# Where two stages of a decoder layer keep their kept weights and sums of x: new offsets mod 512 bytes

## The chip, the cores and the metric

The kernel runs on one core of one Trainium2 chip. The metric is the time of one execution on the device, in microseconds, as the median of several runs. The profile is that of one further execution of the same program.

## What is computed

A decoder layer on 512 tokens of width 1024 in float32: a half-step SwiGLU block, a token mixer (two kinds of recurrent heads), and a second half-step SwiGLU block, each between two RMS norms. The change touches the first matrix product of the two SwiGLU blocks only:

```python
def swiglu_ffn(x, w_in, w_out):
    gate, up = jnp.split(x @ w_in, 2, axis=-1)
    return (jax.nn.silu(gate) * up) @ w_out

x = x + 0.5 * rms_norm(swiglu_ffn(rms_norm(x, norm_pre[l, 0]), ffn1_w_in[l], ffn1_w_out[l]), norm_post[l, 0])
...
x = x + 0.5 * rms_norm(swiglu_ffn(rms_norm(x, norm_pre[l, 2]), ffn2_w_in[l], ffn2_w_out[l]), norm_post[l, 2])
```

`w_in` is 1024 x 5632 (gate and up, 2816 columns each), `w_out` is 2816 x 1024.

## The kernel before, in words

**High and low parts.** Every float32 operand of a matrix product is split into a high part, rounded to the matmul's float32r, and a low part, the rest. A product is then three passes: high x high, high x low, low x high. In `split` (L188) and `cast` (L227) ScalarE writes the high part of a weight (L232) and VectorE the low part (L233); for x, `part` and `sums` do the same (L308, L310, L321, L322).

**The first product by halves.** `x @ w_in` is cut 2 x 2: tokens in halves of 256, the 1024 rows of `w_in` in halves of 512, and for a step t of 256 columns the gate's and the up's columns. From t = 1 on, seven products p1 to p7 with sums and differences of the four quarters stand for eight plain ones. The sums of the weights are made by GpSimd in place (L220), those of x once per block by `sums` (L315). For t = 0 the eight plain products are done: c1 to c4 on the first half of the tokens, e1 to e4 on the second half with the same four weights.

**One product** is `prod` (L496): 24 matmuls at L509, three passes of eight, and each matmul has 128 x 128 weights (the stationary operand, loaded by a LDWEIGHTS) and 256 columns of x (the moving operand). The passes are (weight high, x high), (weight high, x low), (weight low, x high); only c1 has the last two in the other order. Within a pass, the four k of one half of the columns run first and then the four k of the other. `after` (L524) combines what is in PSUM.

**The order** is written out by hand in `ORDER` (L41 to L49). The head (`HEADS`) is c1, c3, c2, c4, p1 of t = 1, e1, e3, e2, p1 of t = 2, p2 of t = 1, e4, p2 of t = 2. Then come p7, p5, p3, p6 of t = 1, the products of t = 2, and from t = 3 to t = 10 a fixed round of seven (p1, p4 of the step before, p3, p5, p7, p6, p2). p4 of t = 10 is done among the second product's matmuls. Transposes of x on TensorE (L288, plain float32) stand inside the head: in the first block between c2 and c4 and between c4 and p1, in the second between c1 and c3 and between c2 and c4. In the first block a transpose of 36 rows of small parameters (L966) stands between the last product of the head and p7 of t = 1.

**Where the operands lie.** Weights go to a ring of four slots in the tile `w`, except those of c1, c3 and c4, which are kept for e1, e3 and e4 in the three tiles `sq` (`self.stay`, chosen by `stay = {"c1": 1, "c3": 2, "c4": 0}` in `ffn_items`). Later the sums of x overwrite these tiles (`self.sq`): tile 0 for p3, tile 1 for p7, tile 2 for p6. The moving operands of all other products lie in the four tiles `xq`. Offsets below are word numbers (4 bytes) mod 128, so mod 512 bytes, in the program's memory: `w` slots begin at 120, all `xq` parts at 40, and the `sq` tiles begin at 56. `LATE` = 112 and `NEAR` = 48 are added to that. So before the change:

| operand | high part at | low part at |
|---|---|---|
| weights in the ring `w` (c2/e2 and p1 to p7) | 120 | 120 |
| kept weight of c1/e1 (`stay[1]`) | 56 | 104 |
| kept weights of c3/e3, c4/e4 (`stay[2]`, `stay[0]`) | 56 | 56 |
| x in `xq` (c1 to c4, e1 to e4, p1, p2, p4, p5) | 40 | 40 |
| sums of x for p3 and p6 (`sq[0]`, `sq[2]`) | 40 | 40 |
| sum of x for p7 (`sq[1]`) | 40 | 56 |

The kept weights are made in `split` with `dst` set; other weights take the next free slot there. `open_ffn` runs once for each block and places all this anew.

Of the kernel before, what the change touches and what calls it, by code (L numbers as in the profile page):

```python
# [16 lines left out]
D = 1024  # L17
# [2 lines left out]
ND = D // P  # L20
NF = FF // P
EPS = 1e-6
RAW, WBUF, PAD, LATE, NEAR = 3, 4, 128, 112, 48
PAIRS = NF // 2
HALF = T // 2
KH = ND // 2
# [18 lines left out]
for _t in range(HEAD, PAIRS):  # L45
    if _t == HEAD:
        ORDER += [("p1", _t), ("p3", _t), ("p5", _t), ("p4", _t - 1)] + [(p, _t) for p in ("p7", "p6", "p2")]
    else:
        ORDER += [("p1", _t), ("p4", _t - 1)] + [(p, _t) for p in ("p3", "p5", "p7", "p6", "p2")]  # L49


class Load:


    def __init__(self, key, src, a, b, ring="raw", depth=3, ahead=3, group=None):
        self.key, self.src, self.a, self.b, self.ring, self.depth, self.ahead = key, src, a, b, ring, depth, ahead
        self.group = group


class Item:  # L60

    def __init__(self, key, loads, rows=None, adds=(), dst=None, then=None, late=None, defer=False):
        self.key, self.loads, self.rows, self.adds, self.dst, self.then, self.late = key, loads, rows, adds, dst, then, late
        self.defer = defer
        self.reads = {key, *(k for pair in adds for k in pair)}


class Layer:  # L70
# [117 lines left out]
    def split(self):  # L188

        nc = self.nc  # L190
        it = self.items.popleft()
        raw = self.raw[it.key]
        _, a, b = raw.shape
        if it.dst:
            w = it.dst()
        else:
            if self.wt is None:
                self.wt = self.wp.tile([P, (2 * D + 128) * WBUF], F32R, name="w")

            n = self.free.popleft()  # L200
            o = PAD + (2 * D + 128) * n - 16 * (it.late if it.late is not None else b == 512)
            w = self.wt[:, o : o + 2 * D].rearrange("p (b k t) -> p b k t", b=2, k=a)
            self.slot[id(w)] = n, w
        hi, lo = self.both(w)
        self.ready.append((w, it.dst is not None))
        rows = it.rows
        if rows is None:
            yield from self.cast(hi, lo, raw, it.defer)
        else:
            for j in range(a):  # L210
                nc.scalar.activation(hi[:, j], raw[:, j], AF.Copy, scale=rows[:, j : j + 1])
            yield
            for j in range(a):
                nc.vector.scalar_tensor_tensor(
                    lo[:, j], raw[:, j], rows[:, j : j + 1], hi[:, j].bitcast(F32), op0=ALU.mult, op1=ALU.subtract
                )
        with self.behind(*self.hold):
            for out, other in it.adds:
                o, c = self.raw[out], self.raw[other]
                nc.gpsimd.tensor_tensor(o, o, c, op=ALU.add)  # L220
        if it.then:
            it.then(raw)
        self.load_due(self.done)
        self.done += 1
        yield
# [76 lines left out]
    def part(self, i, h, src):  # L302

        pv = self.turn(src, h)
        v = slice(i * P, (i + 1) * P)
        dst = self.xq[h][:, :, :, v]
        yield
        self.nc.scalar.copy(dst[:, 0], pv)  # L308
        yield
        self.nc.vector.tensor_tensor(dst[:, 1], pv, dst[:, 0].bitcast(F32), op=ALU.subtract)  # L310
        yield
        self.nc.scalar.copy(self.xf[h][:, :, v], pv)
        yield
# [163 lines left out]
    def open_ffn(self, ctx):  # L477

        hp = self.hpool = ctx.enter_context(self.tc.tile_pool(name=self.name("hp"), bufs=1))
        self.hf = hp.tile([P, NF, T], F32, name=self.name("hf"))  # L480
        self.xf = [self.hf[:, j : j + 2, :].rearrange("p a (b t) -> p (a b) t", t=HALF) for j in (NF - 4, NF - 2)]
        sq = [hp.tile([P, 2 * D + PAD], F32R, tag="s", bufs=3, name=self.name("sq")) for _ in range(3)]
        self.sq = [self.place(t, KH, True) for t in sq]

        part = lambda o: sq[1][:, o : o + D].rearrange("p (k t) -> p k t", k=KH)
        self.sq = [self.both(self.sq[0]), (part(D + LATE), part(0)), self.both(self.sq[2])]
        xq = [self.both(x) for x in self.xq]
        self.stay = [self.place(t, KH) for t in sq]
        self.stay[1] = (self.stay[1][:, 0], sq[1][:, D + NEAR : 2 * D + NEAR].rearrange("p (k t) -> p k t", k=KH))
        self.left = {"p1": xq[0], "p2": xq[1], "p4": xq[3], "p5": xq[2], "p6": self.sq[2], "p7": self.sq[1], "p3": self.sq[0]}  # L490
        self.left.update({"c1": xq[0], "c2": xq[1], "c3": xq[0], "c4": xq[1]})
        self.left.update({"e1": xq[2], "e2": xq[3], "e3": xq[2], "e4": xq[3]})
        self.gs, self.held, self.copies = [], {}, []
        self.hs, self.bank, self.later, self.u, self.q, self.had = deque(), {}, deque(), {}, {}, set()
# [106 lines left out]
    def start(self, norm, xn):  # L601
# [8 lines left out]
        split = self.split()  # L610
        step(q[1][0], q[1][1])
        next(split)
        step(q[1][0])
        next(split)
        step(q[0][0], q[1][0])
        head = deque(HEADS)
# [273 lines left out]
    def ffn_items(self, name, w_in, w_out):  # L890

        made = []
        place = {"p1": "a", "p2": "c", "p3": "d", "p4": "a", "p5": "a", "p6": "a", "p7": "b"}
        place.update({"c1": "a", "c2": "c", "c3": "b", "c4": "d"})
        adds = {}
        for t in range(1, PAIRS):
            if t >= HEAD:
                v1, v3 = ("p1", t), ("p4", t - 1)
            elif t > 1:
                v1, v3 = ("p3", t - 1), ("p6", t - 1)  # L900
            else:
                v1, v3 = ("p1", 1), ("p1", 2)
            for at, o, i in ((("p5", t), "a", "d"), (("p6", t), "a", "c"), (v1, "a", "b"), (v3, "b", "d")):
                adds.setdefault(at, []).append(((name, t, o), (name, t, i)))

        def load(t, r, group=None):
            ring = ("raw", 3) if t % 2 == 0 and r != "c" else ("raw2", 5)
            k, c = int(r in "cd"), int(r in "bd")
            c0 = c * FF + t * 2 * P
            src = w_in[k * 4 * P : (k + 1) * 4 * P, c0 : c0 + 2 * P].rearrange("(k p) f -> p k f", p=P)  # L910
            return Load((name, t, r), src, KH, 2 * P, *ring, 8, group)

        own = {("p1", t): [load(t, r) for r in "abdc"] for t in range(2, PAIRS)}
        own["c1", 0] = [load(t, r, None if (t, r) == (0, "d") else name) for t in range(2) for r in "acbd"]

        stay = {"c1": 1, "c3": 2, "c4": 0}
        for p, t in ORDER:
            if p[0] == "e":
                continue
            dst = (lambda n=stay[p]: self.stay[n]) if p in stay else None  # L920
            made.append(Item((name, t, place[p]), own.get((p, t), ()), None, adds.get((p, t), ()), dst))
        for h in range(2):
            for n, k2, kind in self.outs(h):
                src = w_out[k2 * 2 * P : (k2 + 1) * 2 * P, h * 512 : (h + 1) * 512].rearrange("(k p) d -> p k d", p=P)
                key = (name, "out", h, k2)
                made.append(Item(key, [Load(key, src, 2, 512, "raw2", 5, 8)], then=self.w_sums if kind in "kbs" else None, late=1 + (kind in "kbs")))
                if kind in "kbs":
                    made.append(Item(key, (), late=2, defer=True))
                if h == n == 0:
                    made.append(Item((name, PAIRS - 1, "a"), ()))  # L930
        return made
# [736 lines left out]
```

## Time and profile before

| | us |
|---|---|
| median of 3 runs | 935.06 (934.9 to 936.83) |
| the profiled execution | 934.93 |
| its span | 932.9 |
| TensorE busy | 921.9 (99%) |
| LDWEIGHTS busy | 856.8 (92%) |
| VectorE busy | 759.9 (81%) |
| ScalarE busy | 480.8 (52%) |
| GpSimd busy | 289.4 (31%) |

The profile names engines PE (matmuls), PEld (the loads of their weights, which overlap PE), DVE (VectorE), ACT (ScalarE), POOL (GpSimd), and a line by L and its number. A group of instructions is shown as output<-inputs by tile names, partitions x elements, and a count. Matmuls are pipelined: one that lasts 276 ns in the profile may start 113 ns after the one before it. So the time of a stretch is read from the starts of its first matmul and of the first one behind it, not from the sum of the durations. A row of the timeline ends some 0.16 us behind the start of the next row for the same reason.

### The profile page before, as it was taken

How to read it: one execution, taken by the hardware profiler on the slowest of the kernel's cores; microseconds unless marked ns; L12 is line 12 of the kernel's file. 1: busy time of each engine (PE TensorE's matmuls, PEld its weight loads, DVE VectorE, ACT ScalarE, POOL GpSimd, SP SyncE). 2: the span in 40 equal slices, each digit the busy share in tenths (PEclk: the TensorE clock that was granted, in tenths of full speed). 3: DMA queues.
4: the chain of work that ended last, by engine and by line, in shares of the span. 5: the costliest groups of instructions: out<-in, count | busy, mean ns of one | idle time of the engine just before them, and what ended most of it. 6: DMA issues, size and time to landing. Idle time of an engine off the chain costs nothing.

```text
span 932.9 us, 17378 instructions
## 1 busy us (share of the span) xinstructions
PE 921.9 (99%) x7239; PEld 856.8 (92%) x7239; DVE 759.9 (81%) x899; ACT 480.8 (52%) x653; POOL 289.4 (31%) x225
## 2 busy tenths in 40 slices
PE   9999999999999999999999999999999999999997
PEld 7999999999888879998888888999999999988885
DVE  6798999999768766788766665887999999976874
ACT  7644445444544544987753254853545445544441
POOL 3535555662000028000021301354555565100001
PEclk9999999999999999999999999999999999999999
DMA  9243334332323304432423126214324332233302
GB/s 315 92 136 114 113 92 136 118 110 68 109 95 98 106 1 116 113 91 70 137 69 114 46 90 204 90 27 133 114 91 136 114 113 92 68 115 99 104 23 91
DMA packets 81994, 97.14 MB, mean 104 GB/s; under 512 B 4178, under 2 KB 61558, under 8 KB 81915
## 3 DMA queue, kind: packets, MB, share of 16 engines
q1 hardware_dynamic: 81306, 94.44, 33.3%
q8 instruction: 57, 0.93, 0.4%
q0 software_dynamic: 320, 1.06, 0.3%
q10 hardware_dynamic: 288, 0.52, 0.2%
q14 instruction: 23, 0.18, 0.1%
HBM read 93.90 MB, written 2.11 MB: 103 GB/s over the span
## 4 chain that ended last, share of the span: by engine, by line
PE 61%; DVE 1%; POOL 0%; ACT 0%; issue 0%; DVEq 0%; POOLq 0%; ACTq 0%
PE ps L509 23%; PE ps L129 8%; PE ps L131 8%; PE ps L130 8%; PE ps L454 6%; PE ps L738 3%; PE ps L1167 1%; PE ps L464 1%; PE ps L288 1%; PE ps L1437 0%; PE ps L1405 0%; PE ps L1240 0%; PE ps L1206 0%; PE ps L1407 0%; PE ps L1361 0%; PE ps L1430 0%
## 5 line engine op out<-in xcount | busy, mean ns | idle before, releaser
L233 DVE TENSOR_TENSOR w<-raw,w 128x1024 fp32r<-128x1024 f32 x226 | 374.2, 1666 | 60.8 <-ACT w L232 60.4
L232 ACT CAST w<-raw 128x1024 fp32r<-128x1024 f32 x226 | 235.6, 1051 | 269.8 <-POOL raw L220 92.7
L220 POOL TENSOR_TENSOR raw<-raw,raw 128x1024 f32<-128x1024 f32 x80 | 221.1, 2764 | 175.0 <-DVE w L233 164.5
L509 PE MATMUL ps<-xq,w 128*128 128x256 f32 x2016 | 238.0, 277 | 0.0
L509 PEld LDWEIGHTS ps<-xq,w 128*128 128x128 f32 x2016 | 233.6, 188 | 0.2
L509 PE MATMUL ps<-sq,w 128*128 128x256 f32 x1440 | 171.0, 277 | 0.0
L509 PEld LDWEIGHTS ps<-sq,w 128*128 128x128 f32 x1440 | 167.4, 188 | 0.0
L129 PE MATMUL ps<-w,hs 128*128 128x512 f32 x240 | 93.5, 390 | 0.0
L130 PE MATMUL ps<-w,hs 128*128 128x512 f32 x240 | 93.5, 390 | 0.0
L131 PE MATMUL ps<-w,hs 128*128 128x512 f32 x240 | 93.5, 389 | 0.0
L129 PE MATMUL ps<-w,xq 128*128 128x512 f32 x208 | 83.1, 400 | 0.1
L130 PE MATMUL ps<-w,xq 128*128 128x512 f32 x208 | 81.0, 390 | 0.0
L131 PE MATMUL ps<-w,xq 128*128 128x512 f32 x208 | 81.0, 391 | 0.0
L375 POOL TENSOR_SCALAR col<-col 128x1 f32<-128x1 f32 x24 | 9.7, 403 | 204.3 <-ACT junk L374 204.3
L454 PE MATMUL ps<-xq,w 128*128 128x256 f32 x480 | 55.8, 278 | 0.0
L454 PEld LDWEIGHTS ps<-xq,w 128*128 128x128 f32 x480 | 55.4, 188 | 0.2 <-issue 0.2
L131 PEld LDWEIGHTS ps<-w,hs 128*128 128x128 f32 x240 | 45.1, 188 | 9.4
L129 PEld LDWEIGHTS ps<-w,hs 128*128 128x128 f32 x240 | 45.1, 188 | 8.7
L130 PEld LDWEIGHTS ps<-w,hs 128*128 128x128 f32 x240 | 45.1, 188 | 8.7
L131 PEld LDWEIGHTS ps<-w,xq 128*128 128x128 f32 x208 | 39.0, 188 | 8.7 <-DVE xq L295 0.3
L129 PEld LDWEIGHTS ps<-w,xq 128*128 128x128 f32 x208 | 39.1, 188 | 8.6 <-ACT xq L294 0.7
L130 PEld LDWEIGHTS ps<-w,xq 128*128 128x128 f32 x208 | 39.1, 188 | 7.5
(246 smaller groups left out, 1100.8 us busy)
## 6 DMA issues: line engine op xcount, KB each, us to landing
raw<-in_ffn_w_in_dram SPq DMA_DIRECT2D x88, 512.0 KB, 4.5
raw<-in_ffn_w_out_dram SPq DMA_DIRECT2D x44, 512.0 KB, 3.9
raw<-in_w_mix_in_dram SPq DMA_DIRECT2D x28, 512.0 KB, 4.0
raw<-in_w_mix_out_dram SPq DMA_DIRECT2D x8, 512.0 KB, 3.9
out_dram<-xs SPq DMA_DIRECT2D x8, 256.0 KB, 2.1
xs<-in_x_dram SPq DMA_DIRECT2D x6, 256.0 KB, 6.7
gpost<-in_norm_post_dram SPq DMA_DIRECT2D x3, 512.0 KB
gpre<-in_norm_pre_dram SPq DMA_DIRECT2D x2, 512.0 KB, 4.1
```

What stands on the lines that cost most here:

```text
L129: mm(ps, sh, mh, start=start, stop=False, **kw)
L130: mm(ps, sh, ml, start=False, stop=False, **kw)
L131: mm(ps, sl, mh, start=False, stop=stop, **kw)
L220: nc.gpsimd.tensor_tensor(o, o, c, op=ALU.add)
L232: lambda: nc.scalar.copy(hi, src),
L233: lambda: nc.vector.tensor_tensor(lo, src, hi.bitcast(F32), op=ALU.subtract),
L288: self.nc.tensor.transpose(pt[:, c * P : (c + 1) * P], src[:, k * P : (k + 1) * P], self.ident)
L375: nc.gpsimd.tensor_scalar(m, ss, s2 / D, b, op0=ALU.mult, op1=ALU.add)
L454: mm(ps[:, u0:u1], w[:, a, k, :], self.xop(k, b, u0, u1), start=k + n + m == 0, stop=k == ND - 1 and n == 2, skip_group_check=True,)
L464: self.nc.tensor.matmul(ps[:, :HALF], w[:, a, k, :], self.xop(k, b, 0, HALF), start=m + k == 0, stop=m == 2 and k == ND - 1)
L509: self.nc.tensor.matmul(ps[:, c], wb[b][:, k, v], left[d][:, k, :], start=first and a + n + k == 0, stop=n == 2 and k == KH - 1, skip_grou ...
L738: self.nc.tensor.matmul(out, a[:, x, ka, tok(qa, t)], b[:, y, kb, col(qb)], start=fresh and t + m == 0, stop=stop and m == 2, skip_group_c ...
```

## The change

It moves operands, and nothing else: which instructions run, in which order and on which data stays as it was.

- The kept weights go from the beginning of the `sq` tiles to `FAR` = 64 words behind it, so from 56 to 120, where the ring's weights lie. That of c1/e1 has its high part at 120 and its low part at 104 as before (it changes places with the high part inside the tile).
- All sums of x lie at 40: p7's low part goes from 56 to 40.
- `APART` names p1 of t = 4 and p1 of t = 7. Their weights have the high part in the second half of their slot, at 120, and the low part 16 words ahead of the slot's begin, at 104.

After it, every weight part lies at 120 and every x part at 40, but for four low parts of weights at 104: c1/e1's and those of the two p1.

```diff
-RAW, WBUF, PAD, LATE, NEAR = 3, 4, 128, 112, 48
+RAW, WBUF, PAD, LATE, NEAR, FAR = 3, 4, 128, 112, 48, 64
...
+APART = (("p1", 4), ("p1", 7))
...
-    def __init__(self, key, loads, rows=None, adds=(), dst=None, then=None, late=None, defer=False):
+    def __init__(self, key, loads, rows=None, adds=(), dst=None, then=None, late=None, defer=False, apart=False):
+        self.apart = apart
...
             w = self.wt[:, o : o + 2 * D].rearrange("p (b k t) -> p b k t", b=2, k=a)
+            if it.apart:
+                w = tuple(self.wt[:, v : v + D].rearrange("p (k t) -> p k t", k=a) for v in (o + D, o - 16))
...
-        part = lambda o: sq[1][:, o : o + D].rearrange("p (k t) -> p k t", k=KH)
-        self.sq = [self.both(self.sq[0]), (part(D + LATE), part(0)), self.both(self.sq[2])]
+        part = lambda t, o: t[:, o : o + D].rearrange("p (k t) -> p k t", k=KH)
+        self.sq = [self.both(x) for x in self.sq]
+        self.stay = [(part(t, FAR), part(t, D + FAR)) for t in sq]
+        self.stay[1] = part(sq[1], D + FAR), part(sq[1], NEAR)
         xq = [self.both(x) for x in self.xq]
-        self.stay = [self.place(t, KH) for t in sq]
-        self.stay[1] = (self.stay[1][:, 0], sq[1][:, D + NEAR : 2 * D + NEAR].rearrange("p (k t) -> p k t", k=KH))
...
-            made.append(Item((name, t, place[p]), own.get((p, t), ()), None, adds.get((p, t), ()), dst))
+            made.append(Item((name, t, place[p]), own.get((p, t), ()), None, adds.get((p, t), ()), dst, apart=(p, t) in APART))
```

## The prediction

> **What bounds the kernel now.** I read the page first, for who is busy and what ends the waits of the matmuls that the change touches, then the clock.
>
> ```profile
> span 932.9 us, 17378 instructions
> PE 921.9 (99%) x7239; PEld 856.8 (92%) x7239; DVE 759.9 (81%) x899; ACT 480.8 (52%) x653; POOL 289.4 (31%) x225
> L509 PE MATMUL ps<-xq,w 128*128 128x256 f32 x2016 | 238.0, 277 | 0.0
> L509 PE MATMUL ps<-sq,w 128*128 128x256 f32 x1440 | 171.0, 277 | 0.0
> ```
>
> ```profile
> core 0: 932.9 us, clock 0.998
> ```
>
> TensorE is busy 99% of the span, the products at L509 wait for nobody (0.0 in the last column), and the clock is full. So a nanosecond more or less in the rhythm of these matmuls is a nanosecond of the kernel, 156 products of 24 matmuls. The change alters nothing else. The question is what the place of an operand does to that rhythm. I looked at the timeline of TensorE, first in the middle of the first block, where nothing disturbs it.
>
> ```profile
> 72.88 2.88 PE L509 MATMUL ps<-xq,w 128*128 128x256 f32 x24
> 75.60 2.88 PE L509 MATMUL ps<-sq,w 128*128 128x256 f32 x24
> 78.32 5.60 PE L509 MATMUL ps<-xq,w 128*128 128x256 f32 x48
> 83.76 5.66 PE L509 MATMUL ps<-sq,w 128*128 128x256 f32 x48
> 89.25 8.32 PE L509 MATMUL ps<-xq,w 128*128 128x256 f32 x72
> ```
>
> From start to start a product takes 75.60 - 72.88 = 2.72 us, 113.3 ns a matmul. The row at 83.76 is p7 and p6 of t = 3: 5.49 instead of 5.44, so p7 costs 0.05 more. Now the head of that block.
>
> ```profile
> 12.33 5.90 PE L509 MATMUL ps<-xq,sq 128*128 128x256 f32 x48
> 18.07 2.99 PE L509 MATMUL ps<-xq,w 128*128 128x256 f32 x24
> 20.90 1.04 PE L288 MATMUL ps<-ident,xn 128*128 128x128 f32 x8
> 21.69 2.98 PE L509 MATMUL ps<-xq,sq 128*128 128x256 f32 x24
> 25.31 2.98 PE L509 MATMUL ps<-xq,w 128*128 128x256 f32 x24
> 28.13 5.76 PE L509 MATMUL ps<-xq,sq 128*128 128x256 f32 x48
> 33.72 8.64 PE L509 MATMUL ps<-xq,w 128*128 128x256 f32 x72
> 42.20 2.99 PE L509 MATMUL ps<-xq,sq 128*128 128x256 f32 x24
> 45.03 2.99 PE L509 MATMUL ps<-xq,w 128*128 128x256 f32 x24
> 47.95 0.25 PE L966 MATMUL ps<-ident,rows 36*128 36x36 f32 x1
> 48.13 3.10 PE L509 MATMUL ps<-sq,w 128*128 128x256 f32 x24
> 51.07 2.88 PE L509 MATMUL ps<-xq,w 128*128 128x256 f32 x24
> ```
>
> The row at 33.72 (e2, p1, p2) takes 42.20 - 33.72 = 8.48 for 72 matmuls, 117.8 ns each, or 2.827 a product: **0.107 us slower than the same product later**, though its operands lie where those of the later p1 and p2 lie. So TensorE has two lasting rhythms for one and the same placing, and what came before decides. The durations of one matmul tell them apart:
>
> ```profile
> L509 PE MATMUL ps<-xq,w x69: 276/276/276, 72.9 to 83.3; 128*128 128x256 f32 x69
> L509 PE MATMUL ps<-xq,w x71: 281/281/281, 33.7 to 42.0; 128*128 128x256 f32 x71
> L509 PE MATMUL ps<-xq,sq x8: 281/283/283, 29.9 to 30.8; 128*128 128x256 f32 x8
> L509 PEld LDWEIGHTS ps<-xq,sq x7: 192/192/192, 30.1 to 30.8; 128*128 128x128 f32 x7
> ```
>
> 276 is the fast rhythm and 281 the slow one. The third row is e1's last pass, with the weight's low part at 104: 283, and its loads 192. Where does the rhythm change? The single passes show it.
>
> ```profile
> 29.94 1.12 PE L509 MATMUL ps<-xq,sq 128*128 128x256 f32 x8
> 30.78 3.11 PE L509 MATMUL ps<-xq,sq 128*128 128x256 f32 x25
> 83.76 1.07 PE L509 MATMUL ps<-sq,w 128*128 128x256 f32 x8
> 84.67 1.10 PE L509 MATMUL ps<-sq,w 128*128 128x256 f32 x8
> 85.61 1.09 PE L509 MATMUL ps<-sq,w 128*128 128x256 f32 x8
> ```
>
> Take the last matmul's duration from a row and divide by the steps. e1's odd pass: (1.12 - 0.283)/7 = 120 ns; behind it (3.11 - 0.281)/24 = 117.9, slow, and slow it stays until p7. p7 of t = 3: first pass (1.07 - 0.276)/7 = 113; second pass, with x's low part at 56, 117 to 118; and behind p6 the row at 89.25, quoted above, has (8.32 - 0.276)/71 = 113.3 again.
>
> So **two odd low parts do opposite things**. An odd low part among the weights (104, in c1 and e1) leaves TensorE slow. An odd low part in the moving x (56, in p7) costs 0.05 us and leaves it fast, also when it came in slow: p7 of t = 1 at 48.13 enters slow (its 24 matmuls take 3.10, against 5.66 for 48 at 83.76) and 51.07 is fast (2.88).
>
> **The change part by part.**
>
> Kept weights from 56 to 120. Whether this alone does anything is seen where the slow or the fast rhythm runs from a kept weight into one of the ring.
>
> ```profile
> 596.97 2.98 PE L509 MATMUL ps<-xq,sq 128*128 128x256 f32 x24
> 599.79 2.88 PE L509 MATMUL ps<-xq,w 128*128 128x256 f32 x24
> 602.51 1.03 PE L288 MATMUL ps<-ident,hf 128*128 128x128 f32 x8
> 603.30 3.07 PE L509 MATMUL ps<-xq,sq 128*128 128x256 f32 x24
> ```
>
> In the second block c3 (56) runs into c2 (120) at 599.79, and c2 takes 602.51 - 599.79 = 2.72: fast throughout. In the first, c3 into c2 at 18.07 takes 2.83: slow throughout. 56 and 120, 256 bytes apart, are one and the same to TensorE: nothing for it, between -0.2 and +0.2 us. These ends come from the transposes at L288, after which either rhythm can begin (c4 behind them at 21.69 has a row of 2.98, fast but for some 0.1 of switching; the one at 603.30 has 3.07, another 0.09, slow): c4, or c3 and c2, may change sides, two products at 0.107.
>
> The odd low part of c1/e1 stays at 104, now between 120 and 120 instead of 56 and 56. By the step before that is the same event: 120 ns for eight matmuls, slow behind it. Its four occurrences before all end slow. Bounds: if it acted like p7's, fast behind it. I take the nearest row, 30.78: slow. It removes nothing in the head, then: e3 to p2 of t = 2 stay slow as they are.
>
> p7's low part from 56 to 40 takes away its 0.05 us, and with it **the only event that brings TensorE back** after the head. Then p7 of t = 1 and the 64 products behind it in each block run slow. p7 of t = 1 is slow in two thirds already: 51.07 - 48.13 = 2.94 with some 0.11 of switching behind L966, against 2.83 + 0.11, about nothing. Of the 64, nine are p7, which lose 0.107 but gain 0.053; the others lose 0.107: 55 x 0.107 + 9 x 0.053 = 5.88 + 0.48 = 6.36 us. The two p1 of `APART` have eight matmuls at 120 rather than 117.8: 2 x 0.02 = 0.04. Less 0.01 for p7 of t = 1 in its odd pass (120 against 117.8), that is 6.36 + 0.04 - 0.01 = 6.39 in a block, with two-digit roundings 6.35 to 6.4; for two blocks I take **12.7 us**.
>
> Nothing else moves: same instructions on DVE, ACT, POOL and the queues, and the same tiles written. A slower TensorE only gives them more time. If instead it got faster, what is late next would be the weights of the head:
>
> ```profile
> 36.37 1.22 DVE L233 TENSOR_TENSOR w<-raw,w 128x1024 fp32r<-128x1024 f32 x1 [0.74 <-ACT w L232]
> ```
>
> This low part, done at 37.59, is for p2 of t = 1, which starts at 33.72 + 2 x 2.83 = 39.38: 1.8 us in hand, against 0.5 us that the products before it could gain. That cover holds.
>
> A rule that speaks against all this: the Trainium skill, TensorE: Matmul & The Clock Gate, section "Step-by-step: what each phase is for", says that TensorE has two independent read ports, one for the streaming operand and one for the weights. And SBUF — State Buffer, section "Specifications (TRN2)", speaks only of 16-byte lines, which every offset here keeps. By these the placing would not matter. The trace disagrees: 276, 281 and 283 ns for one shape. It stands as a rival below.
>
> The sum: the profiled execution's 934.93 + 12.7 = 947.6. It lies 0.13 below the median of the runs, so 947.7.
>
> **The rivals.**
>
> *A. An odd weight part brings TensorE back to fast* whenever its neighbours lie at 120, as p7's odd x part does: weight minus x is 120 - 56 = 64 words in p7 and 104 - 40 = 64 here, entered from 80 in both. For it: that likeness. Against it: 56 and 120 are alike in the rows at 599.79 and 18.07, and 104 behind 56 ended slow. It decides at the first matmul behind c1's odd pass. Gain in the first block: c3, c2 (2 x 0.107), e3 to p2 (6 x 0.107), p7 of t = 1 (0.11), nine p7 (0.48), less two odd p1 (0.11): 1.33. In the second c4 and p1 (about 0.2), e1 (0.07), the six, p7 of t = 1 (0.116), the nine, less the two: 1.40. Together -2.7 us, less up to 0.3 for c3, c2 or c4 turning slow behind L288: 932.4. **Faster.**
>
> *B. As A, but L966 leaves the first block slow.* Behind it p7 of t = 1 began slow in the trace (48.13), so 16 products run slow until p1 of t = 4 mends it: 16 x 0.107 + 0.07 = 1.78 back: -0.9, with the same 0.3: 934.2. No change that can be told.
>
> *E. Kept weights leave it slow, the two p1 in the ring make it fast.* Per block 13 x 0.107 + 2 x 0.053 until p1 of t = 4, 0.15 and 0.053 for the two odd p1, less 7 x 0.053: 1.33; 934.93 + 2.7 = 937.6.
>
> *N. The place of an operand does nothing*, the rhythm comes from elsewhere, and the change doesn't do what it is made of. For it: one placing has two rhythms. Against it: p7 alone, of seven products, shows the 0.05 in each round. 934.9.
>
> **How the numbers follow.** Forecast 0.60, E 0.09, N 0.03, B 0.15, A 0.13. About 0.2% (1.9 us) is what a measurement here can tell from no change. Faster by more is A alone: 0.13. Within it are B and N: 0.18. Slower are the forecast and E: 0.69. The forecast's own range is 947.2 to 948.4: two blocks' 0.2 of the transposes and the spread of the runs. To leave no more than 2 in 10 out, the range reaches down over E, N and B to 933.6; A stays out.
>
> **What would show it.** Right: behind e1 (from 31 us) matmuls of 281 in place of 276 to the second product at about 232, L509's mean on the page near 281, p7 and p6 together 5.65, span longer by 12 to 13 with every other stage alike. The odd p1 at 283, and 281 on both sides. Wrong: 276 right behind c1's or e1's odd pass (A, B, then look behind L966), or behind p1 of t = 4 (E). What would upset the sum is an attractor that I have not seen: a stall of TensorE in mid-block that resets the rhythm.

## The result and the profile after

The changed kernel takes **947.78 us** (median of 4 runs, 947.45 to 948.17); the kernel before took 935.94 beside it (934.9 to 937.26). The ratio is 1.0131, 95% interval 1.0119 to 1.0143 (the quotient of the two medians, 1.0127, lies in it). The prediction said 947.7.

The page of the changed kernel (its L513 is L509 of before; in the kernels of the experiments the same line is L509 to L518):

```profile
span 946.1 us, 17380 instructions
PE 934.3 (99%) x7239; PEld 869.3 (92%) x7239; DVE 764.9 (81%) x899; ACT 481.9 (51%) x653; POOL 282.1 (30%) x225
L513 PE MATMUL ps<-xq,w 128*128 128x256 f32 x2016 | 245.7, 281 | 0.0
L513 PE MATMUL ps<-sq,w 128*128 128x256 f32 x1440 | 176.3, 282 | 0.0
```

TensorE does the same 7239 instructions and is busy 12.4 us longer, still waiting for nobody. TensorE, VectorE and GpSimd run their instructions in the order that they had. On ScalarE, contrary to what is said of the change above, four neighbouring pairs have changed places, two in each block: a cast of a weight and a copy behind an odd p1. The loss doesn't come from that: in the first run below these pairs stand as before, and the loss is the same. The mean of a product's matmul went from 277 to 281 and 282. The timeline of TensorE in the changed kernel, first in the head of the first block, then in its middle:

```profile
21.85 3.07 PE L513 MATMUL ps<-xq,sq 128*128 128x256 f32 x24
...
25.55 3.07 PE L513 MATMUL ps<-xq,w 128*128 128x256 f32 x24
28.46 5.83 PE L513 MATMUL ps<-xq,sq 128*128 128x256 f32 x48
34.13 8.64 PE L513 MATMUL ps<-xq,w 128*128 128x256 f32 x72
48.54 3.10 PE L513 MATMUL ps<-sq,w 128*128 128x256 f32 x24
...
85.39 5.82 PE L513 MATMUL ps<-sq,w 128*128 128x256 f32 x48
91.04 8.66 PE L513 MATMUL ps<-xq,w 128*128 128x256 f32 x72
```

p7 and p6 of t = 3 take 91.04 - 85.39 = 5.65 us where they took 5.49, and the three products at 91.04 (one of them an odd p1) have 8.66 where 8.32 stood: slow, as at 34.13, where nothing changed. p7 of t = 1 at 48.54 has the 3.10 that it had. Where the time came from is read off the starts of the first and last product of each block, in the kernel before and in the changed one (the first products of the first block start at 12.33 and 12.45):

```profile
231.09 1.10 PE L509 MATMUL ps<-xq,w 128*128 128x256 f32 x8
...
593.34 0.40 PE L509 MATMUL ps<-xq,sq 128*128 128x256 f32 x2
...
811.70 0.75 PE L509 MATMUL ps<-xq,w 128*128 128x256 f32 x5
```

```profile
12.45 5.94 PE L513 MATMUL ps<-xq,sq 128*128 128x256 f32 x48 [0.24 <-ACT xq L312]
...
237.87 0.87 PE L513 MATMUL ps<-xq,w 128*128 128x256 f32 x6
...
600.13 3.00 PE L513 MATMUL ps<-xq,sq 128*128 128x256 f32 x24
...
824.86 1.34 PE L513 MATMUL ps<-xq,w 128*128 128x256 f32 x10
```

First block: 237.87 - 231.09 - 0.12 = 6.66 us. From there to the second block: 6.79 - 6.78 = 0.01. Second block: 13.16 - 6.79 = 6.37. So the time was lost in both product stages, and nowhere else.

### The profile page after: what moved, and what is told of

The parts are those of the page before. It is cut to its first block, busy times and chain, and to the rows that moved or that the text cites. A ratio compares the mean times of both kernels' runs of the same rounds, so it can differ in the third digit from the quotient of the medians.

```text
span 946.1 us, 17380 instructions
## 1 busy us (share of the span) xinstructions
PE 934.3 (99%) x7239; PEld 869.3 (92%) x7239; DVE 764.9 (81%) x899; ACT 481.9 (51%) x653; POOL 282.1 (30%) x225
## 4 chain that ended last, share of the span: by engine, by line
PE 61%; DVE 0%; POOL 0%; ACT 0%; issue 0%; DVEq 0%; POOLq 0%; ACTq 0%
PE ps L513 23%; PE ps L131 8%; PE ps L133 8%; PE ps L132 8%; PE ps L458 6%; PE ps L742 3%; PE ps L1171 1%; PE ps L468 1%; PE ps L292 1%; PE ps L1441 0%; PE ps L1409 0%; PE ps L1244 0%; PE ps L1210 0%; PE ps L1411 0%; PE ps L1365 0%; PE ps L1434 0%
## 5 line engine op out<-in xcount | busy, mean ns | idle before, releaser
L237 DVE TENSOR_TENSOR w<-raw,w 128x1024 fp32r<-128x1024 f32 x226 | 378.8, 1683 | 69.9 <-ACT w L236 69.3
L224 POOL TENSOR_TENSOR raw<-raw,raw 128x1024 f32<-128x1024 f32 x80 | 213.5, 2669 | 194.6 <-DVE w L237 184.1
L513 PE MATMUL ps<-xq,w 128*128 128x256 f32 x2016 | 245.7, 281 | 0.0
L513 PEld LDWEIGHTS ps<-xq,w 128*128 128x128 f32 x2016 | 241.1, 189 | 0.2
L513 PE MATMUL ps<-sq,w 128*128 128x256 f32 x1440 | 176.3, 282 | 0.0
L513 PEld LDWEIGHTS ps<-sq,w 128*128 128x128 f32 x1440 | 172.4, 189 | 0.0
L458 PE MATMUL ps<-xq,w 128*128 128x256 f32 x480 | 55.8, 279 | 0.0
L458 PEld LDWEIGHTS ps<-xq,w 128*128 128x128 f32 x480 | 55.4, 188 | 0.2 <-issue 0.2
```

The lines of the kernel that those rows point to most:

```text
L237: lambda: nc.vector.tensor_tensor(lo, src, hi.bitcast(F32), op=ALU.subtract),
L458: mm(ps[:, u0:u1], w[:, a, k, :], self.xop(k, b, u0, u1), start=k + n + m == 0, stop=k == ND - 1 and n == 2, skip_group_check=True,)
L513: self.nc.tensor.matmul(ps[:, c], wb[b][:, k, v], left[d][:, k, :], start=first and a + n + k == 0, stop=n == 2 and k == KH - 1, skip_grou ...
```

## The experiments

The **memory theory** is the forecast's: two rhythms last (113.3 and 117.8 ns a matmul, "fast" and "slow" below), an odd low part of x ends fast, an odd low part of a weight ends slow, equal places keep what is there. A part is odd when it lies elsewhere than the other parts of its kind, and a product with one is called odd too. "Ends fast" means that the products behind it run fast, "entered fast" that the product before it did. Rivals: the kept weights at 120 are what costs (W), an odd weight part ends fast (A). Places are words modulo 128.

### One low part of x, alone

```diff
-        self.sq = [self.both(self.sq[0]), (part(D + LATE), part(0)), self.both(self.sq[2])]
+        self.sq = [self.both(self.sq[0]), (part(D + LATE), part(LATE)), self.both(self.sq[2])]
```

> The kernel before with one edit: p7's low part of x at 40 like every other x. Memory theory (two rhythms last; an odd moving part ends in the fast one, an odd weight part in the slow one, equal places keep what is there): the whole loss from this edit alone, +12.6 us, ratio 1.0135; 281 ns from e1 to the end of the products. Rival W (the kept weights at 120 are what costs): 9 x 2 p7 lose their 0.053 each and nothing else happens, -0.95 us, ratio 0.999.

947.72 us (947.33 to 947.88), ratio 1.0136 (1.0122 to 1.0150). Its timeline of TensorE, from p7 of t = 1 on:

```profile
48.33 3.09 PE L509 MATMUL ps<-sq,w 128*128 128x256 f32 x24
51.26 2.99 PE L509 MATMUL ps<-xq,w 128*128 128x256 f32 x24
```

p5 at 51.26 has 2.99, where 2.88 stood behind the odd p7. This one edit, +12.7 us, is as large as the loss of the whole change; W is out.

### The changed kernel with that low part odd again

```diff
         self.sq = [self.both(x) for x in self.sq]
+        self.sq[1] = part(sq[1], D + LATE), part(sq[1], 0)
```

> The changed kernel with one edit undone: p7's low part of x is at 56 again. The kept weights at 120 and the two odd p1 stay. Memory theory: the kept weights cost nothing beyond what the transposes at L288 throw (0 to 0.4 us either way); each odd p1 turns the products behind it slow until p7 of the same t, p4, p3 and p5 at 0.107, its own pass 0.05 and p7 0.07: 0.44 each, four of them +1.8 us, ratio 1.002. Rival W: still +12, ratio 1.013. Rival A (an odd weight part ends fast behind 120): -2.7 us, ratio 0.997.

936.47 us (935.94 to 937.00), ratio 1.0016 (1.0007 to 1.0025): +1.5 of the 1.8 forecast. The odd p1 of t = 4 is the middle product of the row at 88.85:

```profile
88.85 8.48 PE L514 MATMUL ps<-xq,w 128*128 128x256 f32 x72
97.17 2.99 PE L514 MATMUL ps<-sq,w 128*128 128x256 f32 x24
100.00 2.99 PE L514 MATMUL ps<-xq,w 128*128 128x256 f32 x24
102.82 5.72 PE L514 MATMUL ps<-sq,w 128*128 128x256 f32 x48
108.38 3.79 PE L514 MATMUL ps<-xq,w 128*128 128x256 f32 x32
```

p3 and p5 behind it are slow (2.99). p7 with p6 has 5.72, where an entry in the fast rhythm has 5.66: p7 brings TensorE back, and the last row is fast again ((3.79 - 0.276)/31 = 113.4). The odd p1 came in fast, with neighbours at 120, and went out slow: A is out for this place.

### No odd weight part

Against the run before:

```diff
-APART = (("p1", 4), ("p1", 7))
+APART = ()
...
-        self.stay[1] = part(sq[1], D + FAR), part(sq[1], NEAR)
+        self.stay[1] = part(sq[1], D + FAR), part(sq[1], FAR)
```

> As the run before, but no odd weight part at all (c1's and e1's low part at 120, no odd p1): only p7's x is odd. Memory theory: what is fast at e1 stays fast to the end of the head, 6 x 0.107 + 0.05 = 0.7 us in each block that comes out of the transposes fast; one block of two did so before: -0.7 us, between -1.4 and +0.2, ratio 0.9985 to 1.000. If the head is slow for another reason than the odd weight: 0, with 281 from e3 on in both blocks.

933.98 us (933.40 to 934.34), ratio 0.9989 (0.9980 to 0.9997): -1.0 us. The head of its first block:

```profile
27.68 5.60 PE L514 MATMUL ps<-xq,sq 128*128 128x256 f32 x48
33.12 8.32 PE L514 MATMUL ps<-xq,w 128*128 128x256 f32 x72
```

e1 and e3 (27.68) and the next three are fast, where e3 and those three were slow. In this trace c3 and c2 of that block, behind a c1 without an odd pass, are fast too (some 2.72 each where they took 2.83), which the expectation didn't count. The second block came out of its transposes slow and stayed so to p7, as expected.

### Other places for p7's low part of x

```diff
-(part(D + LATE), part(0))
+(part(D + LATE), part(NEAR))   # 104;  part(96): 24;  part(16): 72
```

> The kernel before with p7's low part of x at 104, that is 64 words from the others in place of 16. If any place that differs brings TensorE back: like before, 0 +- 1 us. If the distance counts and 64 words is none: the loss of the first run, +12.6 us. Between them: an odd pass of another rhythm than 120 ns, which the trace will show.

947.24 us (946.97 to 947.78), ratio 1.0132 (1.0118 to 1.0146). Its row for p7 and p6 of t = 3:

```profile
84.41 5.82 PE L509 MATMUL ps<-sq,w 128*128 128x256 f32 x48
```

p7 takes no other time than p6: 104 is to TensorE the same place as 40. Like 56 and 120 for the kept weights, these are 64 words apart, so places repeat every 64 words, 256 bytes, and the 512 of the title are twice the period.

> The kernel before with p7's low part of x at 24: 16 words below the others in place of 16 above. If it is the moving operand that leads to fast: like before, 935 +- 1.5. If it is the direction (-16 slow, as with the weights): 281 behind p7 to the end of the products, 947 to 949.

937.27 us (one run; before 934.95). 24 brings TensorE back too, at a higher price, read from the rows:

```profile
48.91 3.12 PE L509 MATMUL ps<-sq,w 128*128 128x256 f32 x24
51.86 2.88 PE L509 MATMUL ps<-xq,w 128*128 128x256 f32 x24
...
62.74 5.68 PE L509 MATMUL ps<-sq,w 128*128 128x256 f32 x48
68.26 2.88 PE L509 MATMUL ps<-xq,w 128*128 128x256 f32 x24
```

Two products with one p7 take 68.26 - 62.74 = 5.52, 0.08 over 5.44. For x, then, 16 words either way end fast.

> The kernel before with p7's low part of x at 72, 32 words above the others. 64 words did nothing, 16 brought TensorE back to fast. If every shift that is no multiple of 64 does: 935 +- 1.5; if 32 leaves it slow or has a rhythm of its own: 947 to 949 or more, with the pass itself showing which.

947.30 us (one run). 32 words off, the row of p7 and p6 is 5.82 as at 104: slow before, slow behind. How this place acts where TensorE is fast, the run doesn't show.

### Eight places for a weight, entered fast and entered slow

```diff
+TRIES = ((0, 16), (0, 32), (16, 0), (32, 0), (48, 0), (16, 16), (32, 32), (48, 48))
+APART = ({("p1", _t): TRIES[_t - 3] for _t in range(3, 11)}, {("p1", _t): (0, 48) for _t in range(3, 11)})
+APART[1].update({("p3", _t): TRIES[_t - 3] for _t in range(3, 11)})
...
+                h, l = it.apart
+                h, l = (o - 128 + h, o - 128 + l + D) if h <= l else (o - 128 + h + D, o - 128 + l)
```

> The kernel of the run before (kept weights aligned, p7's x odd) with the ring's weights of p1 set apart in every round t = 3 to 10 of the first block, (hi, lo) shifted by (0,16), (0,32), (16,0), (32,0), (48,0), (16,16), (32,32), (48,48) words: each is entered fast. In the second block p1's low part is at -16 in each of these rounds, as in the changed kernel, and p3 behind it takes the same eight shifts: each is entered slow. Memory theory as predicted (any odd weight part leaves TensorE slow, any odd x part leaves it fast): slow behind p1 in all eight rounds of the first block, slow behind p3 in all eight of the second, and p7 makes each fast again. Rival (the direction decides, not the operand): the shifts of +16 end fast. Only the trace counts here; about +4 us if all end slow.

938.29 us (one run; before 934.95). The shift of 48 is that of -16, 64 words on. Shifts are written (high part, low part). Rows of the second block, the tried p3 and p5 behind it, for t = 5 (16,0), 6 (32,0), 7 (48,0) and 9 (32,32):

```profile
698.49 2.97 PE L518 MATMUL ps<-sq,w 128*128 128x256 f32 x24
701.30 2.88 PE L518 MATMUL ps<-xq,w 128*128 128x256 f32 x24
...
717.83 2.97 PE L518 MATMUL ps<-sq,w 128*128 128x256 f32 x24
720.64 2.88 PE L518 MATMUL ps<-xq,w 128*128 128x256 f32 x24
...
737.17 3.02 PE L518 MATMUL ps<-sq,w 128*128 128x256 f32 x24
740.03 2.99 PE L518 MATMUL ps<-xq,w 128*128 128x256 f32 x24
...
776.25 2.99 PE L518 MATMUL ps<-sq,w 128*128 128x256 f32 x24
779.08 2.88 PE L518 MATMUL ps<-xq,w 128*128 128x256 f32 x24
```

And of the first block, the three products with the tried p1 in the middle, for t = 5 and 6 (8.32 is the fast rhythm throughout):

```profile
107.53 8.41 PE L518 MATMUL ps<-xq,w 128*128 128x256 f32 x72
...
126.71 8.32 PE L518 MATMUL ps<-xq,w 128*128 128x256 f32 x72
```

**My rule for weights falls.** In this trace every weight with a part at -16 ends slow, be it the high one, the low one or both. The others don't: a high part at +16 ends fast, at 0.09 us where it came in fast; a high part at +32 costs nothing where it was fast (8.32) and ends fast where it was slow (2.88 at 720.64). Both parts at +32 end fast too where it was slow (2.88 at 779.08). A low part alone at +16 or +32, and both at +16, keep what they find (their rows are not shown). So it isn't "weights slow, x fast"; for weights the direction and the part count.

### Two products at another shift

The changed kernel with its two set-apart p1 at a high part of +32 in place of a low part of -16:

```diff
-for v in (o + D, o - 16))
+for v in (o + D - 96, o - 128))
```

> The changed kernel with one edit: the two p1 set apart (t = 4 and 7) have their high part shifted by +32 words and their low part at 120, in place of the low part at -16. From the run with the eight shifts: this shift changes nothing where TensorE is fast and ends fast where it is slow. So slow from the head to p1 of t = 4 as in the changed kernel, fast for the 48 products behind it: 48 x 0.107 = 5.1 us in a block, 10.3 in both, 947.7 - 10.4 = 937.3, ratio to the kernel before 1.0025. If that shift works only in the surroundings of that run (p7's odd x in each round): 947.7, ratio 1.0135.

937.32 us (936.65 to 937.65), ratio 1.0023 (1.0014 to 1.0032). p1 of t = 4 is the middle of the row at 90.92:

```profile
90.92 8.52 PE L513 MATMUL ps<-xq,w 128*128 128x256 f32 x72
99.28 2.88 PE L513 MATMUL ps<-sq,w 128*128 128x256 f32 x24
102.00 2.88 PE L513 MATMUL ps<-xq,w 128*128 128x256 f32 x24
```

Slow up to it, fast behind it to the end of the products. The other p1, of t = 7, comes in fast and costs nothing. So one weight of each block, p1 of t = 4, with its high part 32 words off and its low part in place, brings the time 10.5 us below the changed kernel's 947.78 (not measured side by side) and leaves 2.4 us of the loss.

### Versions that try to beat both kernels

All x aligned; the three kept weights have both parts shifted by 32, and p1 of every step and p7 of t = 1 their high part. The last p4 stays where it was: `APART` names it, but its weight is made outside the loop that asks `APART`. Against the run before:

```diff
-APART = (("p1", 4), ("p1", 7))
+APART = (("p7", 1), ("p4", 10), *(("p1", _t) for _t in range(1, 11)))
...
-        self.stay = [(part(t, FAR), part(t, D + FAR)) for t in sq]
-        self.stay[1] = part(sq[1], D + FAR), part(sq[1], NEAR)
+        self.stay = [(part(t, FAR + 32), part(t, D + FAR + 32)) for t in sq]
```

> No odd part of 16 words anywhere: x and sums at 40; both parts of the kept weights c1, c3, c4 at 24 (+32), the high part of p1 of every round, of p7 of t = 1 and of the last p4 at +32, all else at 120. If the shift by 32 always ends fast and costs nothing where it was fast: the heads fast but for the products right behind transposes, nine p7 without their 0.053 in a block, -1.5 us a block: 932.0, ratio 0.9968 to the kernel before (-2.6 to -3.1 us by how c1 and c4 fall). If the kept weights at 24 in whole products have a cost of their own, it is read from c1, c3, e1, e3.

934.88 us (934.56 to 935.58), ratio 1.0000 (0.9991 to 1.0008). The rhythm is fast as wanted from e1 on in both blocks, but the first block has new waits:

```profile
57.71 1.98 PE L512 MATMUL ps<-xq,w 128*128 128x256 f32 x16
60.61 1.20 PE L512 MATMUL ps<-xq,w 128*128 128x256 f32 x8 [0.92 <-DVE w L237]
61.65 5.60 PE L512 MATMUL ps<-sq,w 128*128 128x256 f32 x48
```

61.65 - 57.71 = 3.94 us for a product of 2.72: the low part of its weight is late. Upstream of it an addition of weights on GpSimd waits 15.5 us behind the small parameters (8.9 in the changed kernel and in the runs below), and ScalarE's cast waits for GpSimd:

```profile
POOL raw L224 <- DVE col L973: 15.5, 1, 15.5
```

```profile
53.41 1.05 ACT L236 CAST w<-raw 128x1024 fp32r<-128x1024 f32 x1 [5.05 <-POOL raw L224]
```

In this kernel casts of weights stand elsewhere in the order of ScalarE and VectorE than in the kernel before and in the runs below. What in the edit moved them, the eleven weights set apart or the way their parts lie, was not tried alone: the next run changes both. It keeps the order, with two weights of the ring set apart, both parts at +32:

```diff
-for v in (o + D - 96, o - 128))
+for v in (o - 96, o + D - 96))
...
-APART = (("p7", 1), ("p4", 10), *(("p1", _t) for _t in range(1, 11)))
+APART = (("p1", 1), ("p7", 1))
```

> As the run before, but with only two ring weights set apart, p1 and p7 of t = 1, both parts by +32, which leaves the order of the instructions on every engine as it was (in the run before, the casts and differences of some weights stood elsewhere in the queues of ScalarE and VectorE, and TensorE waited 3.5 us for weights in the first block). If those waits came from the order: heads and products fast but for those right behind transposes, 932.0, ratio 0.997. If they came because the faster TensorE outruns the weights: waits for w at L237 again, 934 to 935, ratio 0.999 to 1.000.

The run beside it puts c3 and c4 back:

```diff
-        self.stay = [(part(t, FAR + 32), part(t, D + FAR + 32)) for t in sq]
+        self.stay = [(part(t, FAR + v), part(t, D + FAR + v)) for t, v in zip(sq, (0, 32, 0))]
```

> As the run before with c3 and c4 back at 120, only c1 (and e1, its second use) at 24. If the place of c3 decides on which side TensorE comes out of the transposes in the second block (c3 and c2 slow at 24 in the last run, fast at 120 in four earlier ones): 0.2 us less than the run beside it. If it is chance or no matter: the same within 0.1 us in the trace.

933.50 us (932.94 to 934.72), ratio 0.9986 (0.9977 to 0.9994), and 933.39 us (932.73 to 934.70), ratio 0.9984 (0.9975 to 0.9993). No wait for a weight in either. That alone doesn't clear the faster TensorE, for these heads stayed slow, in whole or in part; but the last run below is fast from e1 on in both blocks, in the order of the kernel before, and has no such wait either. So the order had made the waits. In the second run of the two, e1 at the same place went out slow in the first block and fast in the second (rows of e1 and e3, 48 matmuls):

```profile
28.29 5.82 PE L512 MATMUL ps<-xq,sq 128*128 128x256 f32 x48
```

```profile
608.87 5.71 PE L512 MATMUL ps<-xq,sq 128*128 128x256 f32 x48
```

Both parts at +32 are no sure way, then. c3's place did nothing: c3 and c2 of the second block were slow in both (5.74 us for the two in their traces, against 5.54 in the kernel before). The last run, shown against the first of the two, sets the high part alone, on three weights of a block (the low part of c1 lies at 56, which is 64 words from 120):

```diff
-for v in (o - 96, o + D - 96))
+for v in (o - 96, o + D))
...
-        self.stay = [(part(t, FAR + 32), part(t, D + FAR + 32)) for t in sq]
+        self.stay = [(part(t, FAR), part(t, D + FAR)) for t in sq]
+        self.stay[1] = part(sq[1], FAR + 32), part(sq[1], D + 2 * FAR)
```

> x and sums at 40, and three weights in a block with the high part alone at +32 (24), the low part at 120: c1 (kept, also e1), p1 and p7 of t = 1; the order of the instructions as before. In the runs so far a high part alone at +32 ended fast in all of five slow entries, both parts at +32 only in some. So: c1 to c4 by the transposes, fast from p1 of t = 1 or at the latest behind e1, p7 mends what L966 throws, no p7 at 0.053: per block some 0.64 for the six behind e1, 0.05 to 0.1 for e1, 0.1 for p7 of t = 1, 0.48 for the nine, 1.2 to 1.5; in both 2.4 to 3.0 us, 932.0 to 932.5, ratio 0.997. If the high part at +32 is no surer than both: the head slow in one block or both, as in the last two runs, 933.5, ratio 0.9985.

**932.09 us** (931.58 to 932.22) against 935.48 beside it (934.54 to 937.42), ratio 0.9960 (0.9947 to 0.9974). Its first block:

```profile
21.44 3.07 PE L513 MATMUL ps<-xq,sq 128*128 128x256 f32 x24
...
25.14 3.04 PE L513 MATMUL ps<-xq,w 128*128 128x256 f32 x24
28.02 5.60 PE L513 MATMUL ps<-xq,sq 128*128 128x256 f32 x48
33.46 8.32 PE L513 MATMUL ps<-xq,w 128*128 128x256 f32 x72
...
82.80 5.60 PE L513 MATMUL ps<-sq,w 128*128 128x256 f32 x48
```

c4 comes out of the transposes slow (3.07); p1 behind it begins so and ends fast (3.04); e1 and e3 have 5.60 and p7 with p6 5.60. It is 0.4% faster than the kernel before; against the changed one the medians differ by 947.78 - 932.09 = 15.7 us, not measured side by side.

## Why the prediction was right

- **"The only event that brings TensorE back" removed: 12.7 us.** Shown: the first run is that edit alone and has +12.7; 6.37 in the second block against 6.35 to 6.4. That 947.78 lies within 0.1 us of 947.7 is in part luck: the first block lost 0.27 more than forecast, 12.7 is 2 x 6.39 rounded down, and the kernel before took 935.94 beside the changed one, 0.9 above the time that 12.7 was added to.
- **Kept weights from 56 to 120: nothing.** In the middle of the products that held (the second run's loss is its odd p1). The 0.27 us that the first block lost beyond 6.39 is mostly the step's other half, products changing sides at the transposes: c4 and p1 of t = 1 have 3.07 where 2.98 stood, 0.09 each, and e1 with e3, now entered slow, 5.83 where 5.76 stood. That is 0.25, a little more than the 0.2 allowed, which left out e1. The kept weights don't decide it: with them at 56, c4 was slow in the first run and with p7 at 104, 24 and 72 too (rows of 3.07 to 3.08), and with them at 120 c4 and p1 were fast in the eight-places run (2.98 each).
- **The odd low part of c1 and e1 removes nothing in the head.** Right; without it (third run) the head keeps the rhythm that it gets.
- **The two p1 of `APART`, 0.02 each.** The row at 91.04, with one of them, has 8.66 where three slow products without one have 8.64.
- **p7 of t = 1, about nothing.** 3.10 before and after.
- **Rival A** was right in kind and wrong in place: a weight can bring TensorE back, but at +16 or +32 of its high part, not at -16. The trace of before could not show that; it had no such place. B falls with A for -16, and E too: the odd p1 of t = 4 left TensorE slow in the changed kernel (8.66 at 91.04) and turned it slow in the second run.
- **Rival N** is out: 16 words of one low part moved the kernel by 12.7 us. The Trainium skill, TensorE: Matmul & The Clock Gate, section "Step-by-step: what each phase is for", gives TensorE two independent read ports, one for x and one for the weights. From that one would not expect the 4.5 ns in 113 between the two rhythms; the measurement decides.
- **"No weight is late" if TensorE got faster** held where the order of ScalarE and VectorE stayed (last run), and failed where it didn't (934.88).
- Too broad was the sentence that odd low parts of weights and of x "do opposite things". It described two places, not a rule. The change kept within those two, so the time was right all the same.

## What to carry to other kernels

Where TensorE never waits, compare the start-to-start time of one shape across its stages: 113.3 against 117.8 ns for one and the same matmul is a state, and a state is followed back to the last event that set it. Before such an "irregular" placing is tidied away, look at what runs behind it: here a pass that cost 0.05 us kept 64 products from 0.107 each. And a placing that is to set a state is to be tried from both states, in both directions and for each part; one run with eight places did that.

## What the runs showed of the hardware

- Back-to-back matmuls of 128x256 in this kernel have two lasting rhythms, 113.3 ns (276 each) and 117.8 ns (281), at a granted clock of 0.998 in both kernels' profiles. Operand places repeat every 64 words (256 bytes): 104 acted as 40 did for x, and 120 as 56 for the kept weights.
- x 16 words off either way ends fast, at 0.05 (+16) or 0.08 us (-16) for a product that came in fast; 32 and 64 words off did not end the slow rhythm. Weights at -16 end slow; a high part at +16 ends fast, at 0.09 us where it came in fast (one entry of each kind).
- A weight's high part at +32, its low part in place, cost nothing when fast and ended fast in all seven slow entries that the runs had: p3 in the eight-places run, p1 of t = 4 in both blocks, p1 of t = 1 in both blocks of the 934.88 version, and c1 of the second and p1 of the first block of the last. Both parts at +32 did so in some entries only.
- Open: what in the chip holds the rhythm, and what decides it behind the transposes. c4 of the second block was slow in the changed kernel and fast in the last, from the same place, and c4 of the first block was slow or fast with its weight at 56 and at 120 alike. c3 and c2 of the second block came out of their transposes slow in the three kernels with both parts of c1 at 24, and fast in the others whose traces are told here; why was not tried.
